# A recurrent mixer in chunks: matmuls of two row halves in turns, triangular inversions on GpSimd, a state held per head, and a convolution norm over four tiles

## The chip, the cores and the metric

The kernel runs on one core of one Trainium2 chip. The metric is the device time of one execution in microseconds (us). TensorE (PE in the profile), VectorE (DVE), ScalarE (ACT), GpSimd (POOL) and SyncE (SP, which here only starts DMAs) each work through a queue of their own, strictly in the order in which the program's scheduler has laid it out.

## The reference, cut to what matters

The kernel computes three blocks one after the other on a sequence of 1024 tokens with 1024 channels. The change touches the second block, and there two parts that both feed its output projection.

```python
# recurrent mixer: 8 heads of 64 channels, the state S of a head is 64 x 64
S = S * decay_t + v_t k_t' + (S a_t) b_t'          # one step per token
y_t = S r_t
# convolution part: 512 channels, after a causal convolution of 31 taps
mu  = mean(h, channels); var = mean((h - mu) ** 2, channels)
out = silu((h - mu) * rsqrt(var + 1e-5) * g + b)
```

The kernel replaces the steps over tokens by 8 chunks of 128 tokens, each of two blocks of 64. Within a block the term with `a_t` and `b_t` becomes the inverse of a unit triangular matrix.

## The kernel before, in words

`Block2.rwkv` (what the chunks run in) works in steps `i` from -3 to 8. A step weaves up to five generators, each for another chunk: `rwkv_chain(i)`, `rwkv_out(i-1)`, `rwkv_pre(i+1)`, `rwkv_solve(i+2)`, `rwkv_prep(i+3)`. In step -3 `conv_ln`, the norm of the convolution part, is woven in as well. The weaving only proposes an order: the scheduler of the tile framework fixes the order in each queue.

- `rwkv_prep` loads a chunk's r, k and v from DRAM (L1330), computes decays and scaled operands on ScalarE, GpSimd and VectorE (L1340 to L1388), and multiplies keys and queries of each head pair (L1403; the two heads of a pair lie on rows 0 to 63 and 64 to 127). VectorE masks the product into `gs` (L1405).
- `rwkv_solve` inverts 64 triangular matrices of 16 x 16 per chunk. Eight DMAs bring them from `gs` to DRAM (L1416), one brings them back with a matrix per partition (L1418), GpSimd copies them (L1423) and sets the diagonal (L1424), and 14 rounds follow, each a product (L1428) and a sum (L1430) on VectorE on [64, (15-t) x t] elements: 28 operations on 1120 elements per partition in all, each waiting for the one before. The inverse and its transpose (a copy, L1433) go back to DRAM (L1435, two DMAs) and by 16 DMAs into `tp` (L1439).
- `rwkv_pre` transposes (L1457), turns the 16 x 16 inverses into 64 x 64 ones (L1465, L1473) and applies them (L1480, L1488, L1493).
- `rwkv_chain` carries the state from block to block. The state `Tc` has a head pair in 128 rows by 64 columns. Before the output matmul (L1520) it is written twice scaled: by two operations of VectorE into a block-diagonal tile `Sbd` (L1516), and by one of GpSimd into `Sc` (L1518), which the next state is added to (L1534). L1522 adds the result to `X`, L1528 and L1539 are the matmuls of the state and the output, L1541 the output's copy.
- `rwkv_out` normalizes the output (L1553 to L1564; L1564 is on GpSimd), transposes it (L1568), adds the bonus term (L1572, GpSimd), gates it (L1576, L1577) and stores it.
- `conv_ln` works tile by tile on 128 tokens, 8 times: four transposes into a PSUM bank (L1212), statistics (L1215, L1217), an inverse square root by three Newton steps on a [128, 1] operand (L159 to L168), scaling from PSUM (L1221), transposes back (L1227), gain, SiLU (L1229 to L1234) and a store (L1235).

PSUM has 8 banks: one for `mm`, one for fillers (L172, a bfloat16 matmul that nothing reads), two for `s`, three for `t` (all of `pre` and `conv_ln`), one for `o` (the output of `chain`).

Of the kernel before, what the change touches and what calls it, by code (L numbers as in the profile page):

```python
# [8 lines left out]
F32 = mybir.dt.float32  # L9
# [3 lines left out]
AF = mybir.ActivationFunctionType  # L13
# [4 lines left out]
S = 1024  # L18
# [1112 lines left out]
RW = dict(chain=(9, "010000"), out=(4, "0000"), pre=(15, "100111011010001"), solve=(10, ""), prep=(7, "00010000001"), ln=16, weave=1)  # L1131


class Block2:
# [70 lines left out]
    def conv_ln(self, tmp):  # L1205
        c, nc = self.c, self.c.nc
        g, b = c.vecs["conv_ln_g"], c.vecs["conv_ln_b"]
        for t in range(8):
            ts = slice(t * 128, t * 128 + 128)
            q = c.psum("t")  # L1210
            for i in range(4):
                nc.tensor.transpose(q[:, 128 * i:128 * i + 128], self.cv[:, i, ts], c.ident)  # L1212
            yield
            st = c.sm([128, 6], pool=tmp)
            nc.vector.bn_stats(st, q)  # L1215
            mv = c.sm([128, 2], pool=tmp)
            nc.vector.bn_aggr(mv, st)  # L1217
            rs = c.sm([128, 1], tag="cl", pool=tmp)
# [1075 lines left out]
```

## Time and profile before

| | us |
|---|---|
| median of 3 runs | 3958.29 (3955.69 to 3967.6) |
| the profiled execution's own time | 3958.3 |
| its span, first to last instruction | 3956.6 |
| TensorE busy | 3795.8 (96%) |
| VectorE busy | 2112.9 (53%) |
| ScalarE busy | 1231.0 (31%) |
| GpSimd busy | 540.1 (14%) |
| mean granted TensorE clock | 0.970 of full speed |

A time in the profile counts from the first instruction. The stage of the change runs from about 1112 us (the projections' last matmul) to 1490 us (the first of a long row of matmuls of the output projection). The page's shares are means over the whole kernel, most of which is dense matmuls. The stage has to be read by itself: the busy time of each engine in it, what it idles for, and the order of each queue.

### The profile page before, as it was taken

Reading aid. Unit: us, or ns where it says so; the run is one execution under the profiler, and the core shown is the slowest. Engines: PE = TensorE matmul, PEld = TensorE weight load, DVE = VectorE, ACT = ScalarE, POOL = GpSimd, SP = SyncE. Lnnn points to the kernel's source line nnn. Section 1 sums busy time; section 2 is a strip of 40 time slices with the busy share of each in tenths; the row PEclk is TensorE's granted clock in tenths of the full one; section 3 lists DMA queues with packets and bytes.
Section 4 is the critical chain, followed back from the end, with each engine's and each line's share of the span. In section 5 each row is a group of like instructions: output and inputs, shape, how many; then the busy total and the mean of one; then the engine's idle time right before and its main releaser. Section 6 shows DMA issues by size and latency. Waiting matters only on the chain.

```text
span 3956.6 us, 52689 instructions
## 1 busy us (share of the span) xinstructions
PE 3795.8 (96%) x20288; PEld 3149.7 (80%) x20288; DVE 2112.9 (53%) x4845; ACT 1231.0 (31%) x2521; POOL 540.1 (14%) x825
## 2 busy tenths in 40 slices
PE   7999999799988989999999999999999999999998
PEld 6788888687867777888888888878788888888887
DVE  5356568678977865544444554444433443433155
ACT  4444435542233334222212242333322111121232
POOL 1011124300033411000000011111101211210000
PEclk9999998899978999999999999999999999999999
DMA  5321342431211133111111132111133222211143
GB/s 148 122 65 51 82 138 65 150 114 57 91 55 38 40 104 120 48 54 43 54 43 54 54 121 60 41 58 54 54 107 96 62 64 58 78 49 43 59 150 127
DMA packets 318636, 303.75 MB, mean 77 GB/s; under 512 B 50670, under 2 KB 260402, under 8 KB 318386
## 3 DMA queue, kind: packets, MB, share of 16 engines
q1 hardware_dynamic: 318386, 300.39, 24.5%
q8 instruction: 160, 2.62, 0.3%
q14 instruction: 90, 0.74, 0.1%
HBM read 234.27 MB, written 61.34 MB: 75 GB/s over the span
## 4 chain that ended last, share of the span: by engine, by line
PE 87%; DVE 6%; DMA 3%; ACT 1%; issue 1%; SPq 1%; POOL 1%; DVEq 0%; ACTq 0%; POOLq 0%
PE mm L251 71%; PE s L1809 2%; DMA wraw<-in_w_in_dram 1%; PE s L532 1%; PE t L568 1%; PE o L1831 1%; PE s L1990 1%; PE o L1883 1%; DVE ws L738 1%; PE t L213 1%; PE o L578 1%; PE o L579 1%; SPq L1439 1%; PE s L1403 0%; PE s L531 0%
## 5 line engine op out<-in xcount | busy, mean ns | idle before, releaser
L251 PE MATMUL mm<-ahi,whi 128*128 128x512 f32 x2464 | 967.2, 394 | 0.0
L251 PE MATMUL mm<-alo,whi 128*128 128x512 f32 x2464 | 965.5, 392 | 1.3 <-DVE alo L218 1.3
L251 PE MATMUL mm<-ahi,wlo 128*128 128x512 f32 x2464 | 964.3, 392 | 1.9 <-DVE wlo L184 1.9
L184 DVE TENSOR_TENSOR wlo<-wraw,whi 128x1024 fp32r<-128x1024 f32 (+2 forms) x300 | 358.2, 1231 | 361.1 <-PE mm L251 337.6
L251 PEld LDWEIGHTS mm<-ahi,wlo 128*128 128x128 f32 x2464 | 464.7, 189 | 98.4 <-DVE wlo L184 2.6
L251 PEld LDWEIGHTS mm<-ahi,whi 128*128 128x128 f32 x2464 | 465.8, 189 | 96.3 <-issue 0.4
L251 PEld LDWEIGHTS mm<-alo,whi 128*128 128x128 f32 x2464 | 465.1, 189 | 96.7 <-DVE alo L218 2.2
L183 ACT ACTIVATE whi<-wraw 128x1024 fp32r<-128x1024 f32 (+2 forms) x300 | 302.9, 1055 | 760.2 <-DMA wraw<-in_w_ff_dram 315.1
L251 PE MATMUL mm<-whi,ahi 128*128 128x512 f32 (+2 forms) x1088 | 400.2, 371 | 21.1 <-ACT whi L183 8.2
L251 PE MATMUL mm<-whi,alo 128*128 128x512 f32 (+2 forms) x1088 | 399.0, 368 | 1.6 <-DVE alo L218 1.6
L251 PE MATMUL mm<-wlo,ahi 128*128 128x512 f32 (+2 forms) x1088 | 400.4, 368 | 0.1
L251 PEld LDWEIGHTS mm<-whi,ahi 128*128 128x128 f32 x1088 | 206.6, 190 | 57.1 <-ACT whi L183 8.7
L1683 DVE TENSOR_TENSOR xm<-xm,mm 128x512 f32<-128x512 f32 x256 | 173.6, 684 | 119.8 <-PE mm L251 119.5
L251 PEld LDWEIGHTS mm<-wlo,ahi 128*128 128x128 f32 x1088 | 206.5, 190 | 35.2 <-issue 3.8
L251 PEld LDWEIGHTS mm<-whi,alo 128*128 128x128 f32 x1088 | 206.0, 189 | 35.2 <-issue 2.5
L251 PE MATMUL mm<-whi,ah 128*128 128x512 f32 x512 | 202.3, 395 | 0.0
L251 PE MATMUL mm<-wlo,ah 128*128 128x512 f32 x512 | 202.1, 395 | 0.0
L251 PE MATMUL mm<-whi,al 128*128 128x512 f32 x512 | 202.1, 395 | 0.0
L1170 DVE SCALAR_TENSOR_TENSOR cva<-cvh,vecs,cva 128x1022 f32<-128x1022 f32 (+29 forms) x120 | 145.4, 1262 | 0.2
L1665 DVE TENSOR_TENSOR fr<-fr 128x512 f32<-128x512 f32 x64 | 44.4, 694 | 154.0 <-ACT fr L1664 154.0
L207 POOL TENSOR_SCALAR x<-x,rT 128x1024 f32<-128x1024 f32 x16 | 20.9, 1307 | 752.3 <-PE mm L251 676.8
L1815 POOL TENSOR_SCALAR mS<-mS,s 128x256 f32<-128x256 f32 x128 | 60.8, 478 | 405.2 <-DVE s L1814 337.8
(576 smaller groups left out, 5761.2 us busy)
## 6 DMA issues: line engine op xcount, KB each, us to landing
wraw<-in_w_in_dram SPq DMA_DIRECT2D x41, 1024.0 KB
wraw<-in_w_ff_dram SPq DMA_DIRECT2D x32, 1024.0 KB
wraw<-in_w_in_dram SPq DMA_DIRECT2D x59, 512.0 KB
wraw<-in_w_out_dram SPq DMA_DIRECT2D x24, 1024.0 KB
gv<-go SPq DMA_DIRECT2D x32, 256.0 KB
vl<-gv SPq DMA_DIRECT2D x16, 512.0 KB
wraw<-in_w_proj_a_dram SPq DMA_DIRECT2D x8, 1024.0 KB
wraw<-in_w_proj_b_dram SPq DMA_DIRECT2D x8, 1024.0 KB
```

Source lines behind the costliest of these rows:

```text
L183: nc.scalar.activation(hi, src, AF.Copy)
L184: nc.vector.tensor_tensor(lo, src, hi.bitcast(F32), op=OP.subtract)
L213: nc.tensor.transpose(q[:, 128 * j:128 * j + 128], xn[:, (k + j) * 128:(k + j + 1) * 128], self.ident)
L251: nc.tensor.matmul(out, lhs[a][:, kl, ls], rhs[b][:, kr, rs], start=first and n == 0, stop=last and n == tot - 1)
L532: nc.tensor.matmul(q[:, :b - a], self.Q[0:64, h, qs], kl, start=False, stop=True)
L568: nc.tensor.transpose(t[:w, (2 * j + s) * 128:(2 * j + s + 1) * 128], Ps[s][:, k:k + w], c.ident)
L578: nc.tensor.matmul(o[:, :256], v[:w, 0:128], ph[:w, sl], start=first, stop=last, skip_group_check=True)
L1170: nc.vector.scalar_tensor_tensor(a[:, 30 - j:], h[:, 0:994 + j], wj, a[:, 30 - j:], op0=OP.mult, op1=OP.add)
L1665: nc.vector.tensor_tensor(r, r, r, op=OP.mult)
L1683: nc.vector.tensor_tensor(xm[t][:, ns], xm[t][:, ns], q, op=OP.add)
L1809: nc.tensor.matmul(q[:, :256], qk[:, a, qcol], qk[:, b, kcol], start=n == 0, stop=n == 2)
L1815: nc.gpsimd.tensor_scalar(S_, S_, r, 1.0, op0=OP.mult, op1=OP.mult)
```

## The change

Five edits, all in `Block2`:

1. Matmuls of two row halves are issued in turns, each half into a PSUM bank of its own (L1336, L1403, L1465, L1480, L1488 and L1493; L1344, L1411, L1474, L1491, L1500 and L1507 in the changed kernel).
2. The 28 operations of the inversion and the transposing copy go from VectorE to GpSimd (L1428, L1430, L1433; now L1437, L1439, L1442).
3. The block-diagonal `Sbd` goes. `Sc` is computed by VectorE and used as it is: four matmuls over 128 rows become eight over 64, with one bank for each of the two heads of a pair. The sum with `X` and the copy of the output are split in two as well.
4. `conv_ln` works on four tiles at a time: ScalarE copies the transposed tile to SBUF, the inverse square root is taken once for four tiles on a [128, 4] operand, and the scaling reads SBUF. In the weaving it has 24 places in step -3 in place of 16.
5. Banks: `t` has two in place of three, `o` two in place of one.

```diff
@@ conv_ln
-        for t in range(8):
...
-            c.rsqrt(rs, mv[:, 1:2], 1.0, 1e-5, "cl", tmp)
-            x = tmp.tile([128, 512], F32, tag="O", name=c.nm("lnx"), bufs=2)
-            nc.vector.tensor_scalar(x, q, mv[:, 0:1], rs, op0=OP.subtract, op1=OP.mult)
+        for t0 in (0, 4):
+            xs = []
+            mv = c.sm([128, 4, 2], tag="cmv", bufs=2, pool=tmp)
+            for k in range(4):
...
+                nc.scalar.activation(x, q, AF.Copy)
+                st = c.sm([128, 6], pool=tmp)
+                nc.vector.bn_stats(st, q)
+                nc.vector.bn_aggr(mv[:, k], st)
...
+            nc.vector.tensor_copy(vr, mv[:, :, 1])
+            c.rsqrt(rs, vr, 1.0, 1e-5, "cl", tmp)
+            for k, x in enumerate(xs):
...
+                nc.vector.tensor_scalar(x, x, mv[:, k, 0:1], rs[:, k:k + 1], op0=OP.subtract, op1=OP.mult)
@@ rwkv_prep
-            for s in range(2):
-                rs = slice(64 * s, 64 * s + 64)
-                q = c.psum("s")
-                for pr in range(4):
+            qq = [c.psum("s") for _ in half]
+            for pr in range(4):
+                for q, rs in zip(qq, half):
                     nc.tensor.matmul(q[:, 128 * pr:128 * pr + 128], kb[rs, pr, 2 * b:2 * b + 2], va[rs, pr, 1 + 4 * b:3 + 4 * b],
                                      start=True, stop=True)
+            for s, q in enumerate(qq):
                 TT(gs[:, b, s:8:2], r4(q), m, op=OP.mult)
@@ rwkv_solve
-            nc.vector.tensor_tensor(x, mv[:, t + 1:16, t:t + 1].to_broadcast(sh), tv[:, t:t + 1, 0:t].to_broadcast(sh),
+            nc.gpsimd.tensor_tensor(x, mv[:, t + 1:16, t:t + 1].to_broadcast(sh), tv[:, t:t + 1, 0:t].to_broadcast(sh),
                                     op=OP.mult)
-            nc.vector.tensor_tensor(tv[:, t + 1:16, 0:t], tv[:, t + 1:16, 0:t], x, op=OP.add)
+            nc.gpsimd.tensor_tensor(tv[:, t + 1:16, 0:t], tv[:, t + 1:16, 0:t], x, op=OP.add)
...
-        nc.vector.tensor_copy(lTT.rearrange("p (j t) -> p j t", t=16), tj)
+        nc.gpsimd.tensor_copy(lTT.rearrange("p (j t) -> p j t", t=16), tj)
@@ rwkv_pre
-        for b in range(2):
-            ca = slice(64 * b, 64 * b + 64)
-            q = c.psum("t")
-            for h in range(8):
-                nc.tensor.matmul(q[Bh(b), H(h)], gs[Bh(b), b, h, ca], T16[Bh(b), h], start=True, stop=True)
+        qq = [c.psum("t") for _ in range(2)]
+        for h in range(8):
+            for b, q in enumerate(qq):
+                nc.tensor.matmul(q[Bh(b), H(h)], gs[Bh(b), b, h, 64 * b:64 * b + 64], T16[Bh(b), h], start=True, stop=True)
+        for b, q in enumerate(qq):
             TT(ET[Bh(b), :, Bh(b)], h8(q[Bh(b)]), self.mLow[Bh(b)].unsqueeze(1).to_broadcast([64, 8, 64]), op=OP.mult)
@@ rwkv_chain
-                S = self.Sbd[b]
                 f = self.ff[j][:, :, b:b + 1]
-                for s in range(2):
-                    TT(S[H(s), :, H(s)], self.Tc[H(s)], f[H(s)].to_broadcast([64, 4, 64]), op=OP.mult)
                 Sc = tmp.tile([128, 4, 64], F32, tag="Sc", name=c.nm("Sc"), bufs=2)
-                nc.gpsimd.tensor_tensor(Sc, self.Tc, f.to_broadcast([128, 4, 64]), op=OP.mult)
-                for pr in range(4):
-                    nc.tensor.matmul(o[:, 128 * pr:128 * pr + 128], va[:, pr, 2 + 2 * b:4 + 2 * b], S[:, pr], start=pr == 0,
-                                     stop=False, skip_group_check=True)
-                TT(VU[b][Bh(b)], o[Bh(b)], X[Bh(b)], op=OP.add)
+                TT(Sc, self.Tc, f.to_broadcast([128, 4, 64]), op=OP.mult)
+                for pr in range(4):
+                    for s in range(2):
+                        nc.tensor.matmul(o[s][:, 64 * pr:64 * pr + 64], va[H(s), pr, 2 + 2 * b:4 + 2 * b], Sc[H(s), pr],
+                                         start=pr == 0, stop=False, skip_group_check=True)
+                for s in range(2):
+                    TT(hs(VU[b][Bh(b)], s), r4(o[s][Bh(b)]), hs(X[Bh(b)], s), op=OP.add)
@@ second_block
-        c.set_banks(mm=[0], f=[1], s=[2, 3], t=[4, 5, 6], o=[7])
+        c.set_banks(mm=[0], f=[1], s=[2, 3], t=[4, 5], o=[6, 7])
```

How the queues change is shown at three places. The first is GpSimd in a middle step, around the copy that begins an inversion. Before, only the copy (L1423) and the diagonal (L1424) of an inversion stood between operations of `prep`, `chain` and `out`:

```order
L1377 TENSOR_TENSOR ws_10869<-rk_12664,rk_12665 128x512
L1385 TENSOR_TENSOR ws_10873<-ws_10873,ws_10871 128x512
L1423 COPY ws_10872<-ws_10870 64x256
L1424 MEMSET ws_10872 64x16
L1345 TENSOR_SCALAR ws_10871<-rk_13112,vecs_625 128x128 x4
L1518 TENSOR_TENSOR Sc_13104<-Tc_12856,ff_11925 128x256
L1572 TENSOR_TENSOR y_12690<-y_12690,tp_11283 128x512
L1340 TENSOR_SCALAR ws_10871<-ws_10871 128x512
L1423 COPY ws_10872<-ws_10870 64x256
L1564 TENSOR_TENSOR O_12653<-O_12653,s_2559_13245 128x512
L1424 MEMSET ws_10872 64x16
```

Now the product and the sum of the 14 rounds stand there, with `out`'s normalization (L1582) among them:

```order
L1354 TENSOR_SCALAR ws_10871<-rk_13081,vecs_625 128x128
L1439 TENSOR_TENSOR ws_10872<-ws_10872,ws_10874 64x14
L1354 TENSOR_SCALAR ws_10871<-rk_13081,vecs_625 128x128 x3
L1437 TENSOR_TENSOR ws_10874<-ws_10870,ws_10872 64x26
L1439 TENSOR_TENSOR ws_10872<-ws_10872,ws_10874 64x13x2
L1437 TENSOR_TENSOR ws_10874<-ws_10870,ws_10872 64x36
L1439 TENSOR_TENSOR ws_10872<-ws_10872,ws_10874 64x12x3
L1437 TENSOR_TENSOR ws_10874<-ws_10870,ws_10872 64x44
L1439 TENSOR_TENSOR ws_10872<-ws_10872,ws_10874 64x11x4
L1437 TENSOR_TENSOR ws_10874<-ws_10870,ws_10872 64x50
L1582 TENSOR_TENSOR O_12151<-O_12151,s_2471_12758 128x512
L1439 TENSOR_TENSOR ws_10872<-ws_10872,ws_10874 64x10x5
```

Sixteen more operations of the same inversion and the bonus term of `out` (L1590) follow before the transposing copy, and only then `prep` of the next chunk.

The second place is SyncE's queue in a middle step (`tp` are the inverses, `gs` the products, `ws` the matrices by partition, `rk` the loads of a later chunk). Before:

```order
L1435 DMA lane<-ws_10872 64x256
L1435 DMA lane<-kb_10868 64x256
L1439 DMA tp_11283<-lane 16x8x16 x16
L1578 DMA catT<-y_13137 128x4x128
L1416 DMA lane<-gs_10867 16x8x16 x8
L1418 DMA ws_10870<-lane 64x256
```

Now, in the step of chunk 4:

```order
L1444 DMA lane<-ws_10872 64x256
L1444 DMA lane<-kb_10868 64x256
L1448 DMA tp_11221<-lane 16x8x16 x16
L1596 DMA catT<-y_12197 128x4x128
L1425 DMA lane<-gs_10866 16x8x16 x4
L1336 DMA rk_13080<-p2T 128x4x128
L1336 DMA rk_13081<-p2T 128x4x128
L1427 DMA ws_10870<-lane 64x256
```

The load that starts an inversion (L1427) stands behind the write-back and the 16 loads of the inversion before it. Of chunks 3 to 7, two had that load ahead of those 16 loads before (chunks 5 and 7, L1418 ahead of L1439); now all five have it behind. For chunk 2 it is ahead now and was behind before.

The third place is TensorE, where `prep` and `pre` of two chunks meet. Before, with the four groups of L1403 of a chunk (one bank `s` each):

```order
L1403 MATMUL s_12610<-va_10864,kb_10868 128x128 x4
L1576 MATMUL mm_12575<-lora,wup 128x128 x4
L1473 MATMUL t_12503<-Pc_12458,ws_10872 64x64 x16
L172 LDWEIGHTS reset
L172 MATMUL f_12522<-reset 128x384
L1403 MATMUL s_12616<-va_10864,kb_10868 128x128 x4
L1403 MATMUL s_12622<-va_10864,kb_10868 128x128 x4
L1488 MATMUL t_12529<-Pc_12520,ws_10870 64x64 x8
L1493 MATMUL t_12544<-X_2420_12299,Pc_12520 64x64 x8
L1488 MATMUL t_12582<-Pc_12520,ws_10870 64x64 x8
L1403 MATMUL s_12628<-va_10864,kb_10868 128x128 x4
```

Now, with the two groups of L1474 (banks `t`) and the first matmuls of L1411:

```order
L1474 MATMUL t_12707<-tp_11221,gs_10867 64x64 x8
L1536 MATMUL o_12775<-Sc_12776,va_10865 128x64 x4
L1411 MATMUL s_13022<-va_10864,kb_10868 128x128
L1474 MATMUL t_12708<-tp_11221,gs_10867 64x64 x8
L172 LDWEIGHTS reset
L172 MATMUL f_12726<-reset 128x384
L1545 MATMUL mm_12811<-ws_10870,ws_10874 64x64
L1556 MATMUL o_12774<-ws_10870,gs_10867 64x64 x4
L1411 MATMUL s_13023<-va_10864,kb_10868 128x128
L1545 MATMUL mm_12811<-ws_10870,ws_10874 64x64 x7
```

The product of keys and queries (L1411) alternates between its two banks at 77 of 127 neighbouring places, the low-rank product of `prep` (L1344) at 26 of 63. The two groups of L1474 still stand one behind the other, eight and eight, as L1465 did, and so do those of L1491 and L1507 in every chunk. L1500 alternates at 120 of 127 places.

## Rows read from the trace of the kernel before

**Rows 1.** The page: the span of the profiled execution.

```profile
span 3956.6 us, 52689 instructions
```

**Rows 2.** Busy time by stretch: us, then each engine, PEclk, DMA share, GB/s.

```profile
1110.00:1240.00 130.00, 100.58 (x658) 80.82 (x656) 91.27 (x242) 48.61 (x118) 55.91 (x74) 0.65 0.19 48
1240.00:1400.00 160.00, 149.21 (x1973) 126.26 (x1972) 136.88 (x328) 61.99 (x139) 62.63 (x83) 0.97 0.20 45
```

**Rows 3.** Chain of waits at the end of the stage: start us, us, what.

```profile
1490.83 9.37 PE mm L251 x28
```

**Rows 4.** SyncE's queue in order of time, whole stage: start us, us, what.

```profile
1178.98 0.49 SPq L1435 DMA_DIRECT2D lane<-ws  x1
...
1212.65 0.45 SPq L1435 DMA_DIRECT2D lane<-ws  x1
...
1241.09 0.45 SPq L1435 DMA_DIRECT2D lane<-ws  x1
...
1353.38 0.45 SPq L1435 DMA_DIRECT2D lane<-ws  x1
...
1356.31 8.11 SPq L1439 DMA_DIRECT2D tp<-lane  x16
...
1364.99 3.79 SPq L1416 DMA_DIRECT2D lane<-gs  x8
1369.93 0.47 SPq L1418 DMA_DIRECT2D ws<-lane  x1
...
1395.52 1.75 SPq L1416 DMA_DIRECT2D lane<-gs  x4
...
1434.93 0.45 SPq L1435 DMA_DIRECT2D lane<-ws  x1
```

**Rows 5.** Costly lines of VectorE, 1110 to 1490: busy us, mean ns | idle us.

```profile
L1430 DVE TENSOR_TENSOR ws<-ws,ws 64x14 f32<-64x14 f32 (+6 forms) x112 | 30.4, 271 | 2.5
L1428 DVE TENSOR_TENSOR ws<-ws,ws 64x14 f32<-64x14 f32 (+6 forms) x112 | 27.4, 245 | 13.0 <-POOL ws L1423 10.8
...
L1516 DVE TENSOR_TENSOR Sbd<-Tc,ff 64x256 f32<-64x256 f32 x30 | 16.5, 551 | 0.4
...
L164 DVE SCALAR_TENSOR_TENSOR cl<-cl,cl 128x1 f32<-128x1 f32 x24 | 10.4, 432 | 0.1
```

**Rows 6.** GpSimd in order of time, 1340 to 1410: start us, us, what.

```profile
1343.35 0.63 POOL L1518 TENSOR_TENSOR Sc<-Tc,ff 128x256 f32<-128x256 f32 x1 [1.37 <-DVE Tc L1534]
...
1359.42 1.40 POOL L1345 TENSOR_SCALAR ws<-rk,vecs 128x128 f32<-128x128 f32 x4
...
1372.39 0.60 POOL L1423 COPY ws<-ws 64x256 f32<-64x256 f32 x1 [1.61 <-DMA ws<-lane]
1373.17 1.04 POOL L1564 TENSOR_TENSOR O<-O,s 128x512 f32<-128x512 f32 x1 [0.18 <-DVE s L168]
...
1375.75 0.12 POOL L1424 MEMSET ws<- 64x16 f32 x1
1375.90 1.04 POOL L1361 TENSOR_TENSOR ws<-ws,s 128x512 f32<-128x512 f32 x1
...
1388.19 1.26 POOL L1572 TENSOR_TENSOR y<-y,tp 128x512 f32<-128x512 f32 x1 [0.78 <-ACT y L1570]
```

**Rows 7.** VectorE in order of time, one operation of an inversion.

```profile
1375.93 1.05 DVE L1430 TENSOR_TENSOR ws<-ws,ws 64x14 f32<-64x14 f32 x1
```

**Rows 8.** The copy ahead of the inversions (L1423): ns min/median/max, first and last start us.

```profile
L1423 POOL COPY ws<-ws x8: 597/608/1214, 1153.1 to 1406.7; 64x256 f32<-64x256 f32 x8
```

**Rows 9.** TensorE in order of time, 1354 to 1361.

```profile
1354.81 1.14 PE L1480 MATMUL t<-ws,gs 64*64 64x64 f32 x16
...
1356.74 1.15 PE L1473 MATMUL t<-Pc,ws 128*64 128x64 f32 x32
...
1359.05 1.71 PE L1403 MATMUL s<-va,kb 64*128 64x128 f32 x16
```

**Rows 10.** Waits of TensorE, 1110 to 1490: us in total, times, longest us.

```profile
PE mm L1568 <- POOL O L1564: 6.7, 1, 6.7
```

More of the change, by code (lines that the diff above doesn't have):

```diff
@@ L1130 @@
 FN = 384
-RW = dict(chain=(9, "010000"), out=(4, "0000"), pre=(15, "100111011010001"), solve=(10, ""), prep=(7, "00010000001"), ln=16, weave=1)
+RW = dict(chain=(9, "010000"), out=(4, "0000"), pre=(15, "100111011010001"), solve=(10, ""), prep=(7, "00010000001"), ln=24, weave=1)
 class Block2:
@@ L1331, in rwkv_prep @@
         sg, a, cs, kk, e, ei, ea, t1, t2, t3 = self.wk[:10]
-        for x, rows, b in ((sg, slice(0, 64), "w0"), (a, slice(64, 128), "a0")):
-            q = c.psum("s")
-            for pr in range(4):
-                ps = slice(128 * pr, 128 * pr + 128)
+        half = [slice(0, 64), slice(64, 128)]
+        qq = [c.psum("s") for _ in half]
+        for pr in range(4):
+            ps = slice(128 * pr, 128 * pr + 128)
+            for q, rows in zip(qq, half):
                 nc.tensor.matmul(q[:, ps], self.wup[rows, 0, ps], self.lwa[rows, js], start=True, stop=True)
+        for x, q, b in ((sg, qq[0], "w0"), (a, qq[1], "a0")):
             for pr in range(4):
@@ L1476, in rwkv_pre @@
             yield
[L1477 to L1478 removed]
+            if i == 0:
+                qq = [c.psum("t") for _ in range(2)]
                 for h in range(8):
[L1480 to L1482 removed]
+                    for b, q in enumerate(qq):
+                        nc.tensor.matmul(q[Bh(b), H(h)], gs[Kh(b), b, h, Kh(b)], VU[b][Kh(b), H(h)], start=True, stop=True)
+                for b, q in enumerate(qq):
+                    nc.scalar.activation(x1[Bh(b)], q[Bh(b)], AF.Copy)
+                    yield
         X = self.X[j] = tmp.tile([128, 512], F32, tag="X", name=c.nm("X"), bufs=2)
[L1484 to L1487 removed]
+        qq = [c.psum("t") for _ in range(2)]
+        for h in range(8):
+            pr, s = h // 2, h % 2
+            for b, q in enumerate(qq):
                 nc.tensor.matmul(q[H(s), H(pr)], VU[b][Bh(b), H(h)], cur[Bh(b), H(h)], start=True, stop=True)
+        for b, q in enumerate(qq):
             nc.scalar.activation(va[:, :, 3 + b], q[:, 0:256].rearrange("p (r t) -> p r t", r=4), AF.Copy)
             yield
[L1491 to L1492 removed]
+        qq = [c.psum("t") for _ in range(2)]
+        for h in range(8):
+            for b, q in enumerate(qq):
                 nc.tensor.matmul(q[Bh(b), H(h)], cur[Bh(b), H(h)], x1[Bh(b), H(h)], start=True, stop=True)
+        for b, q in enumerate(qq):
             nc.scalar.activation((X if j or b else VU[b])[Bh(b)], q[Bh(b)], AF.Copy)
@@ L1538, in rwkv_chain @@
             for h in range(8):
-                nc.tensor.matmul(o[Kh(b), H(h)], gs[:, b, h, cr], VU[b][:, H(h)], start=first and h == 0, stop=h == 7,
-                                 skip_group_check=True)
-            nc.scalar.activation(O[Kh(b)], o[Kh(b)], AF.Copy)
+                pr, s = h // 2, h % 2
+                nc.tensor.matmul(o[s][Kh(b), 64 * pr:64 * pr + 64], gs[:, b, h, cr], VU[b][:, H(h)], start=first and pr == 0,
+                                 stop=pr == 3, skip_group_check=True)
+            for s in range(2):
+                nc.scalar.activation(hs(O[Kh(b)], s), r4(o[s][Kh(b)]), AF.Copy)
             yield
```

77 lines of the change are left out of this document (32 added, 45 removed).

## The prediction

> **What bounds the kernel now.** I read the page first: the span is 3956.6 us [rows 1], and 3958.3 us is the same execution's own time, equal to the median of the three runs (3958.29), so every sum below is made against it. Its shares say nothing of this change, since dense matmuls fill most of the span. So the table of busy times by stretch comes next [rows 2]. From 1240 to 1400 us VectorE is busy 136.88 of 160 us and TensorE 149.21 (its ends are modelled, so it is less full than that), GpSimd only 62.63. In the 130 us ahead of it the granted clock is 0.65: TensorE is at 1.2 GHz for much of the time, while it waits for VectorE and GpSimd; later it is 0.97, nearly always 2.4 GHz. The stage ends where the long row of dense matmuls begins, at 1490.83 [rows 3].
>
> Third I read SyncE's queue, since a chunk's inversion goes out and in through it, and take the start of the write-back (L1435) as the clock of the stage [rows 4]. Call it T. It starts at 1179.0 for chunk 0, 1212.7, 1241.1 and so on, and 1434.9 for chunk 7: 36.6 us per chunk. From T(7) to the end of the stage are 55.9 us.
>
> **The change, part by part.**
>
> *Inversions leave VectorE.* Their 224 operations take 30.4 + 27.4 us there [rows 5], 7.2 us of each chunk. In the middle VectorE is busy 136.88 / 160 x 36.6 = 31 us per chunk, so this is a real relief.
>
> *Inversions on GpSimd.* No row shows a small tensor-tensor operation there, so I bound it. Below: a fill of 16 elements takes 0.12 us. Above: 256 elements in a copy take 0.60. An operation with two inputs takes 1.04 on 512 [rows 6]. The line through 0.60 and 1.04 has 1.72 ns per element and 0.16 us fixed. 28 operations with 1120 elements: 28 x 0.16 + 1120 x 0.00172 = 6.4 us, and 28 gaps of 0.05 (0.03 stands between the fill and what follows) make 7.8. I take that line because it passes between the bounds and fits both kinds. The bounds are 3.4 and 16.8 us. Copy and fill ahead: 0.72. The queue puts other work among the 28: four scalings for the next chunk (1.40), out's normalization (1.04) and bonus sum (1.26), 3.7 in all.
>
> *The shared port.* GpSimd's operation at 1375.90 to 1376.94 [rows 6] and a 14-element sum of VectorE from 1375.93, which took 1.05 us [rows 7], ended together: the small one waited for the big one. So 28 small reads of SBUF beside VectorE's sums of two SBUF operands will meet. I estimate 2.0 us per inversion, a 0.7 us operation met one time in ten. The Trainium skill, page "SBUF — State Buffer", section "Who interferes with whom", says that a VectorE instruction with two SBUF inputs and a GpSimd instruction that reads SBUF exclude each other fully; the trace agrees with the 1.05 us above.
>
> The Trainium skill, "GPSIMD Engine Reference", section 3.1, speaks against this part: elementwise work with two inputs is about twice as slow on GpSimd. By that rule one operation costs twice VectorE's 0.245 to 0.271 us, an inversion 14.4 us in place of 9.8, and the time would be 7 x 4.6 = 32 us above my sum, 3950; no run here shows it.
>
> *The new loop.* The queue order sets what is late next. The load that starts chunk j+1's inversion stands behind chunk j's write-back and its 16 loads. From rows [rows 4, 6]: T to the first of the 16, 1356.31 - 1353.38 = 2.93; the 16, 8.11; to the next issue 0.57; four DMAs of `gs` 1.75; two loads of a later chunk, 2 x 0.45 like their neighbours; from the end of the `gs` DMAs (1368.78) to the load at 1369.93, 1.15; to GpSimd's copy at 1372.39, 2.46. Together 17.9. Then GpSimd: 0.72 + 7.8 + 3.7 + 2.0 = 14.2. The loop is **32.1 us per chunk**, for the five from T(2) to T(7). prep's own operations on GpSimd fit into the 17.9: it is busy 62.63 / 160 x 36.6 = 14.3 per chunk, less 4.3 for two state scalings (0.63), out's two and the copy, so 10.0.
>
> *The start.* T(0): the copy ran at 1153.1 [rows 8], behind the norm's work in GpSimd's queue, and it still does. Then came 26 us to T(0); now there are 0.7 + 7.8 + 2.0 and 10.0 of the next prep, 20.5 us, with two tiles of the norm and waits on top. I leave T(0) at 1179, within 10 us either way. T(1) = T(0) + 33.7 as before. Chunk 2's load no longer waits for the 16, and its inversion follows at once: 10.0 + 0.7 + 7.8 + 2.0 + 0.6 = 21.1, so T(2) = 1233.8. T(7) = 1233.8 + 5 x 32.1 = 1394.3, **40.6 us** ahead of 1434.9.
>
> *The norm over four tiles.* It removes three quarters of the Newton steps; the 24 of L164 alone took 10.4 us [rows 5] for single elements. All lie in the first 70 us, where T(0) hangs on GpSimd's queue: I count nothing. If that cover is gone, T(0) comes up to 10 us earlier; the two `t` banks can take as much back.
>
> *State per head.* VectorE loses two operations of 0.55 per block [rows 5] and gains one, and a split sum; ScalarE gains a copy. About 1 us per chunk, hidden by the loop; without that cover it is 8 us in all.
>
> *Row halves.* In the trace L1473 alternates column halves: 32 instructions in 1.15 us, where L1480, with its half fixed for eight matmuls, takes 1.14 for 16; L1403 takes 1.71 for 16 [rows 9]. Turns halve the time. But the order gives L1474, L1491 and L1507 no turns, L1411 77 of 127, L1344 26 of 63. At 0.107 us each L1403's 256 instructions are 27 us and L1336's 128 are 14: 27 x 0.61 / 2 + 14 x 0.41 / 2 = 11 us of TensorE in the whole stage instead of the 48 that full turns would give (with 9 each for L1465, L1480 and L1493). By the same rows the matmuls of one chunk need 27 us at full clock (116 instructions of 128 columns at 0.107, 128 of 64 at 0.071, 160 in turns at 0.036), fillers apart. That was under the loop before and stays under 32.1, so I count nothing; up to 11 us if TensorE sets the pace.
>
> *The tail* after T(7) keeps its 55.9. **Sum: 3958.3 - 40.6 = 3918 us.** The bounds of the small operation alone give 3880 (3.4 us in place of 7.8 and no meeting at the port, in the six inversions from T(1) to T(7)) and 3981 (16.8 in place of 7.8, in all seven).
>
> **The rivals.**
>
> *The loads cost less than I think* and the engines set the pace: VectorE needs 31 - 7.2 - 1 = 23 us, TensorE 26 and its fillers. Steps of 28 and a T(0) 10 us earlier put T(7) at 1223.8 + 140 = 1363.8, 71 us ahead: 3887. For it: SyncE idles much of the time. Against it: the queue order.
>
> *TensorE stalls.* Its transposes of the output wait for GpSimd (6.7 us once [rows 10]), and in two or three steps the normalization now stands a dozen places into an inversion. TensorE waits in order, its clock falls to 1.2 GHz as in the first stretch (0.65 [rows 2]), and pre, which follows the inversion, runs at half speed. Steps of 38, about the 38.8 that these five took before, with T(2) unchanged at 1241: T(7) = 1431, 3954: no change.
>
> *Slower: GpSimd becomes the bound through the port.* If half the 28 operations wait for a 0.7 us operation, the 2.0 becomes 9.8: loop 40, T(1) and T(2) 8 later each. T(7) = 1249.8 + 200 = 1450, 15 late, and VectorE's own sums wait as well, some 3 us: 3976. It decides from 40.6 / 7 = 5.8 us more per inversion, a mean of 0.56 us per operation, inside my bounds.
>
> *The turns don't happen* (the order says so for three of the six lines) takes TensorE's relief from the second case; it leaves the sum as it is.
>
> **How the numbers follow.** A measurement of this kernel tells 0.3% (12 us) from no change. The forecast, 3918, has 0.50; engine-bound, 3887, 0.22; the stall, 3954, 0.16; slower, 3976, 0.12. The first two are faster by more than 12 us: 0.72; same 0.16; slower 0.12. The range reaches from the lower bound of the small operation, which takes in the second case, past the third: 3880 to 3962. What lies above is the fourth.
>
> **What would show it.** Right: write-backs about 32 us apart from chunk 2 on, each copy 18 us behind the write-back before it; 28 operations of 0.2 to 0.35 us on GpSimd; VectorE's busy time in the middle down by a quarter; T(7) near 1394. L1411 faster, L1474 not. Wrong: small operations at 0.5 us or more; GpSimd waiting for ScalarE or VectorE inside an inversion; a clock clearly below 0.97 after chunk 1; copies that start as soon as GpSimd is free, which would mean that the loads don't set the pace.

## The result, and the profile after

The changed kernel takes 0.9941 of the time before (95% interval 0.9924 to 0.9957), 23 us less of 3959; its executions lie between 3927.8 and 3944.62 us; one in a slow state, 7285.15 us, is left out. The profiled one took 3944.62 us, its span against [rows 1]:

```profile
span 3942.9 us, 52905 instructions
```

So the profile has 13.7 us of the 23 to show. The stage itself shortened by more. Three windows of busy time (us, PE, PEld, DVE, ACT, POOL, then PEclk, DMA share, GB/s): the dense matmuls ahead of the stage, with the same code in both kernels, and the stage from its first matmul of prep to the end, first before,

```profile
779.00:1110.00 331.00, 325.98 (x1450) 268.93 (x1451) 275.53 (x457) 93.77 (x169) 16.94 (x18) 0.99 0.28 93
1117.00:1491.00 374.00, 317.42 (x3433) 264.44 (x3433) 278.42 (x704) 140.59 (x310) 132.89 (x172) 0.83 0.23 58
```

then after, with the two stretches of [rows 2] between them:

```profile
779.00:1110.00 331.00, 321.27 (x1416) 264.73 (x1417) 271.00 (x453) 94.92 (x169) 16.13 (x17) 0.97 0.29 96
1110.00:1240.00 130.00, 107.31 (x899) 88.06 (x899) 79.02 (x146) 57.47 (x135) 84.19 (x157) 0.74 0.23 59
1240.00:1400.00 160.00, 154.32 (x1951) 128.27 (x1948) 105.66 (x211) 61.16 (x146) 99.80 (x222) 0.90 0.22 50
1125.00:1481.00 356.00, 315.94 (x3550) 260.61 (x3549) 214.58 (x432) 146.11 (x334) 193.48 (x389) 0.83 0.24 61
```

By 1110 the profiled execution of the changed kernel is 34 dense matmuls (7.6 us, at 325.98 / 1450 each) behind, before any changed line has run. The stage takes 356 us in place of 374. VectorE lost 64 us, GpSimd gained 61. TensorE has hardly fewer busy microseconds (315.94 against 317.42) though the halves now take turns, and in the middle its clock is lower than before (0.90 against 0.97). So nearly all of the 18 us is idle time of TensorE, 57 us before and 40 after.

The clock of the stage that the prediction used, the write-back of each chunk, in SyncE's queue (start us, us, what), chunks 2 to 7, with the next inversion's load where the loop is read:

```profile
1242.75 0.45 SPq L1444 DMA_DIRECT2D lane<-ws  x1
...
1273.19 0.45 SPq L1444 DMA_DIRECT2D lane<-ws  x1
...
1288.72 0.47 SPq L1427 DMA_DIRECT2D ws<-lane  x1
...
1307.88 1.35 SPq L1444 DMA_DIRECT2D lane<-ws  x1
...
1338.10 0.45 SPq L1444 DMA_DIRECT2D lane<-ws  x1
...
1372.16 0.45 SPq L1444 DMA_DIRECT2D lane<-ws  x1
...
1400.89 0.45 SPq L1444 DMA_DIRECT2D lane<-ws  x1
```

From T(2) to T(7) are 158.1 us, 31.6 per chunk (28.7 to 34.7 in the single steps). GpSimd in order of time, a copy that waits for its load and the last inversion from end to end:

```profile
1291.28 0.60 POOL L1432 COPY ws<-ws 64x256 f32<-64x256 f32 x1 [3.41 <-DMA ws<-lane]
...
1391.50 0.21 POOL L1437 TENSOR_TENSOR ws<-ws,ws 64x14 f32<-64x14 f32 x1
...
1396.22 0.28 POOL L1437 TENSOR_TENSOR ws<-ws,ws 64x56 f32<-64x56 f32 x1
1396.58 0.30 POOL L1439 TENSOR_TENSOR ws<-ws,ws 64x56 f32<-64x56 f32 x1
...
1400.65 0.22 POOL L1439 TENSOR_TENSOR ws<-ws,ws 64x14 f32<-64x14 f32 x1
```

What follows T(7) is where the forecast parts from the trace. TensorE in order of time: the first matmuls of chunk 7 that need its inversion (L1474) run only at 1425.29, and until then TensorE works through chunk 6, chain and dense matmuls, with one gap of 0.49 us. Behind these rows stands the end of the stage, in the chain of waits (start us, us, what).

```profile
1417.22 1.14 PE L1507 MATMUL t<-X,Pc 64*64 64x64 f32 x16 [0.49 <-ACT va L1502]
...
1425.29 1.14 PE L1474 MATMUL t<-tp,gs 64*64 64x64 f32 x16
```

```profile
1480.81 19.32 PE mm L251 x78
```

In the kernel before 55.9 us lay between T(7) and 1490.83 [rows 3, 4]; here it is 1480.81 - 1400.89 = 79.9. TensorE's busy time in these two stretches, before and after (columns of the windows above), shows that the 24 us more are work and not waits: it is idle for 11.7 us in either.

```profile
1434.00:1491.00 57.00, 45.35 (x527) 38.45 (x526) 27.44 (x69) 20.86 (x38) 10.05 (x9) 0.90 0.30 89
1400.00:1481.00 81.00, 69.32 (x779) 56.75 (x776) 35.80 (x84) 29.49 (x55) 9.50 (x11) 0.86 0.27 89
```

The lines of TensorE that the change touches (busy us, mean ns | idle us before), after:

```profile
L1411 PE MATMUL s<-va,kb 64*128 64x128 f32 x256 | 30.9, 344 | 8.8 <-DVE cl L166 6.0 <-DVE cl L1226 2.8
L1536 PE MATMUL o<-Sc,va 64*128 64x64 f32 x240 | 25.9, 292 | 0.2 <-DVE Sc L1533 0.2
L1556 PE MATMUL o<-ws,gs 128*64 128x64 f32 x256 | 25.9, 255 | 0.0
L1474 PE MATMUL t<-tp,gs 64*64 64x64 f32 x256 | 20.7, 247 | 0.0
L1491 PE MATMUL t<-ws,gs 64*64 64x64 f32 x256 | 20.3, 233 | 0.0
L1545 PE MATMUL mm<-ws,ws 128*64 128x64 f32 x240 | 18.0, 261 | 4.1 <-DVE ws L1539 4.1
L1507 PE MATMUL t<-X,Pc 64*64 64x64 f32 x256 | 17.9, 221 | 1.8 <-ACT va L1502 1.8
L1344 PE MATMUL s<-lora,wup 64*128 64x128 f32 x128 | 14.4, 317 | 0.1
L1500 PE MATMUL t<-Pc,ws 64*64 64x64 f32 x256 | 5.6, 224 | 0.5 <-DVE Pc L1485 0.5
```

and those of them in the kernel before that had most to change (the others there: L1465 22.5, L1480 20.3, L1493 17.8, L1488 10.9, L1528 11.9 us):

```profile
L1403 PE MATMUL s<-va,kb 64*128 64x128 f32 x256 | 38.2, 333 | 2.6 <-DVE gs L1405 1.1 <-DVE cl L168 0.9 <-DVE kb L1388 0.6
L1336 PE MATMUL s<-lora,wup 64*128 64x128 f32 x128 | 23.4, 332 | 0.0
L1539 PE MATMUL o<-ws,gs 128*64 128x64 f32 x256 | 20.9, 236 | 0.0
L1520 PE MATMUL o<-Sbd,va 128*128 128x128 f32 x120 | 19.5, 309 | 0.0
```

The six lines of the halves fell from 133.1 to 109.8 us. The three of the chain (L1520, L1528, L1539; now L1536, L1545, L1556) rose from 52.3 to 69.8. So the chain took back 17.5 of the 23.3 us. Only 6.4 of the 17.5 lie in the line whose matmuls doubled (L1520, now L1536); the other two lines have as many matmuls as before.

### The profile page after: what moved, and what is told of

Same layout as the page of the kernel before. It is cut to its first block, busy times and chain, and to the rows that moved or that the text cites. A ratio compares the mean times of both kernels' runs of the same rounds, so it can differ in the third digit from the quotient of the medians.

```text
span 3942.9 us, 52905 instructions
## 1 busy us (share of the span) xinstructions
PE 3804.1 (96%) x20408; PEld 3155.7 (80%) x20408; DVE 2049.9 (52%) x4573; ACT 1237.7 (31%) x2545; POOL 602.4 (15%) x1041
## 4 chain that ended last, share of the span: by engine, by line
PE 89%; DVE 5%; DMA 3%; ACT 1%; issue 1%; POOL 1%; SPq 0%; DVEq 0%; ACTq 0%; POOLq 0%
PE mm L251 72%; PE s L1827 2%; DMA wraw<-in_w_in_dram 1%; PE s L532 1%; PE t L568 1%; PE s L2008 1%; PE o L1849 1%; PE o L1901 1%; DVE ws L738 1%; PE t L213 1%; PE t L1483 1%; PE o L578 1%; PE o L579 1%; PE s L531 0%; PE t L1474 0%
```

## The experiments

The four parts of the change were first tried one at a time in the kernel before (the banks go with the state per head). Then the state per head and the inversions were each taken out of the changed kernel, and its fillers and the order of its turns were varied; the norm and the halves were not taken out of it. Two theories stand against each other in what was expected. T: TensorE sets the step of the changed kernel. I: the loop of write-back, loads and inversion still does. In the table us is (ratio - 1) x 3960. The stage's length and TensorE's busy time are those of each profile's window, as above; idle is the rest of the window; "at 1.2 GHz" is 2 x (1 - PEclk) x length, good to 4 us. The last column is the mean step of the write-backs from T(2) to T(7). A ratio is to executions of the kernel before taken beside that kernel. The changed kernel was not run again beside its variants, so a difference between two rows compares two ratios.

| kernel | ratio to before (95%) | us | stage | TensorE busy | idle | PEclk | at 1.2 GHz | step |
|---|---|---|---|---|---|---|---|---|
| before | 1 | 0 | 374 | 317 | 57 | 0.83 | 127 | 38.8 |
| changed | 0.9941 (0.9924 to 0.9957) | -23 | 356 | 316 | 40 | 0.83 | 121 | 31.6 |
| b_inv: before + inversions | 0.9949 (0.9933 to 0.9966) | -20 | 364 | 322 | 42 | 0.81 | 138 | 35.0 |
| b_norm: before + norm | 0.9975 (0.9961 to 0.9989) | -10 | 367 | 311 | 56 | 0.84 | 117 | 31.7 |
| b_state: before + state per head | 1.0094 (1.0075 to 1.0113) | +37 | 407 | 354 | 53 | 0.78 | 179 | 39.6 |
| b_rows: before + halves in turns | 0.9925 (0.9907 to 0.9942) | -30 | 345 | 289 | 56 | 0.88 | 83 | 32.4 |
| b_t2: before, two t banks | 1.0000 (0.9989 to 1.0012) | 0 | 373 | 313 | 60 | 0.84 | 119 | 33.3 |
| b_rowsnorm: before + halves + norm | 0.9970 (0.9958 to 0.9982) | -12 | 363 | 305 | 58 | 0.83 | 123 | 32.3 |
| a_nostate: changed, old chain | 0.9900 (0.9883 to 0.9918) | -40 | 338 | 289 | 49 | 0.87 | 88 | 33.4 |
| a_invdve: changed, inversions on VectorE | 1.0031 (1.0019 to 1.0043) | +12 | 386 | 341 | 45 | 0.80 | 154 | 36.8 |
| a_turns: changed, turns held in order | 1.0011 (0.9999 to 1.0023) | +4 | 386 | 293 | 93 | 0.81 | 147 | 35.1 |
| a_nofill: changed, no fillers | 1.0057 (1.0042 to 1.0073) | +23 | 401 | 322 | 79 | 0.75 | 200 | 38.5 |
| s_fill: b_state, more fillers | 1.0071 (1.0059 to 1.0083) | +28 | 409 | 358 | 51 | 0.81 | 155 | 38.9 |
| ns_fill: a_nostate, more fillers | 0.9992 (0.9983 to 1.0001) | -3 | 375 | 328 | 47 | 0.83 | 128 | 38.0 |

**The inversions alone (b_inv).** The operations of L1428, L1430 and L1433 of the kernel before:

```
-            nc.vector.tensor_tensor(x, ...)
-            nc.vector.tensor_tensor(tv[:, t + 1:16, 0:t], ...)
-        nc.vector.tensor_copy(lTT..., tj)
+            nc.gpsimd.tensor_tensor(x, ...)
+            nc.gpsimd.tensor_tensor(tv[:, t + 1:16, 0:t], ...)
+        nc.gpsimd.tensor_copy(lTT..., tj)
```

> The kernel before with nothing changed but the inversions, which run on GpSimd. Theory T (in the changed kernel TensorE's own work sets the step of about 33 us, and the inversions only release it up to there): the loop of the write-backs falls from 36.6 to about 32 us, but TensorE, which here has the halves in blocks, needs 33 us or more a step, so the time falls by 5 to 15 us. Theory I (the loop of the inversions still sets the pace in the changed kernel, and the other parts add nothing): the whole gain of the change, 23 us, is here.

Measured: 20 us less (13 to 27), near the 23 of the whole change, as theory I has it; but what the other parts gave (next runs) is far from nothing, so this run alone decides neither. TensorE's idle time in the stage fell from 57 to 42 us. The step of the write-backs fell to 35.0 us only, not to the 32 that was expected, T(2) and T(7) being

```profile
1246.94 0.45 SPq L1435 DMA_DIRECT2D lane<-ws  x1
...
1421.99 0.45 SPq L1435 DMA_DIRECT2D lane<-ws  x1
```

**The norm alone (b_norm).** `conv_ln` and the weaving number as in the change:

```
-        for t in range(8):
+        for t0 in (0, 4):
+            for k in range(4):
...
+            c.rsqrt(rs, vr, 1.0, 1e-5, "cl", tmp)
...
- ln=16
+ ln=24
```

> The kernel before with nothing changed but the convolution's norm over four tiles (and its 24 turns). The prediction counts it as nothing: within 6 us of the kernel before, with the first write-back within 10 us of 1179. Rival: its Newton steps were on VectorE's path at the start, and the time falls by 10 us.

Measured: 10 us less, the rival's figure. The term was not nothing. That the Newton steps were on the path is not shown by it: T(0) comes at 1171.32, within the 10 us that the prediction allowed, and TensorE's idle time in the stage is what it was (57 and 56 us); its busy time is 6 us less.

**The state per head alone (b_state).** `rwkv_chain` and the banks as in the change:

```
-                    nc.tensor.matmul(o[:, 128 * pr:128 * pr + 128], va[:, pr, ...], S[:, pr], ...)
+                    for s in range(2):
+                        nc.tensor.matmul(o[s][:, 64 * pr:64 * pr + 64], va[H(s), pr, ...], Sc[H(s), pr], ...)
...
-        c.set_banks(mm=[0], f=[1], s=[2, 3], t=[4, 5, 6], o=[7])
+        c.set_banks(mm=[0], f=[1], s=[2, 3], t=[4, 5], o=[6, 7])
```

> The kernel before with nothing changed but the state per head (two o banks, two t banks). The prediction counts it as nothing: within 6 us. Rivals: VectorE's 1 us per chunk is on the path and the time falls by 8 us; or the third t bank was needed, and pre, which takes its PSUM there, makes it slower by 5 to 15 us.

Measured: 37 us more, outside every expectation; the profiled execution, 3989.16 us, is the shortest of its six, so its profile shows less than that. Its busy time by stretch:

```profile
1220.00:1240.00 20.00, 20.00 (x269) 16.71 (x268) 17.47 (x55) 10.06 (x25) 8.56 (x17) 1.00 0.26 58
1240.00:1260.00 20.00, 20.00 (x151) 17.16 (x151) 18.34 (x50) 3.76 (x7) 4.37 (x7) 0.52 0.19 47
1260.00:1280.00 20.00, 20.00 (x177) 16.75 (x177) 6.71 (x12) 5.19 (x16) 5.75 (x9) 0.50 0.14 17
1280.00:1300.00 20.00, 20.00 (x113) 14.96 (x114) 13.58 (x42) 4.53 (x9) 4.36 (x5) 0.50 0.08 20
1300.00:1320.00 20.00, 20.00 (x230) 16.61 (x231) 8.95 (x16) 3.94 (x9) 2.70 (x5) 0.78 0.09 18
```

For these 100 us TensorE is busy all the time, and for 68 of them (2 x (1 - PEclk) x 20 in each window) the granted clock is 1.2 GHz. At full clock the same work takes a little over half as long by the price below, so this one stretch costs up to 34 us. The list of waits names none for TensorE from 1220 to 1310: nothing kept it from working. Its last idle time before the fall lies between 1200 and 1220, where it is busy for 17.77 of 20 us. Its order of time shows what it ran as the clock fell (start us, us, what), and the price of L1462's 16 matmuls there, 1.80 and 1.97 us, where the changed kernel's same line at full clock (L1474, above) takes 1.14:

```profile
1237.37 1.10 PE L1518 MATMUL o<-Sc,va 64*128 64x64 f32 x8
...
1240.43 1.80 PE L1462 MATMUL t<-tp,gs 64*64 64x64 f32 x16
...
1297.25 1.97 PE L1462 MATMUL t<-tp,gs 64*64 64x64 f32 x16
```

**The halves in turns alone (b_rows).** The loops of `rwkv_prep` and `rwkv_pre` as in the change, one of six:

```
-        for b in range(2):
-            q = c.psum("t")
-            for h in range(8):
-                nc.tensor.matmul(q[Bh(b), H(h)], gs[Bh(b), b, h, ca], T16[Bh(b), h], ...)
+        qq = [c.psum("t") for _ in range(2)]
+        for h in range(8):
+            for b, q in enumerate(qq):
+                nc.tensor.matmul(q[Bh(b), H(h)], gs[Bh(b), b, h, 64 * b:64 * b + 64], T16[Bh(b), h], ...)
```

> The kernel before with nothing changed but the loops over row halves written in turns. Theory T: in the kernel before the loop of the inversions, 36.6 us, stands above TensorE's work, so less TensorE work gives nothing, within 6 us. Rival: TensorE is on the path already, and its 11 us less are 11 us of time.

Measured: 30 us less, more than the whole change. TensorE is busy 28 us less, and 44 us fewer of the stage run at 1.2 GHz; its idle time is what it was. The six lines of the halves have 26 of the 28: they take 107.2 us in place of 133.1. So TensorE was on the path of the kernel before, against theory T's reading of it and against the prediction. The step of the write-backs fell too, from 38.8 to 32.4 us, with the inversions still on VectorE:

```profile
1239.56 0.45 SPq L1438 DMA_DIRECT2D lane<-ws  x1
...
1401.63 0.45 SPq L1438 DMA_DIRECT2D lane<-ws  x1
```

**Two t banks (b_t2).**

```
-        c.set_banks(mm=[0], f=[1], s=[2, 3], t=[4, 5, 6], o=[7])
+        c.set_banks(mm=[0], f=[1], s=[2, 3], t=[4, 5], o=[7])
```

> The kernel before with nothing changed but the banks of PSUM: two t banks in place of three. Two readings of the 37 us by which the state per head alone made the kernel slower. Banks: its third t bank was what pre needed, so this kernel loses 20 to 37 us as well, and the granted clock is at 1.2 GHz for some 180 us of the stage in place of 133. Chain: the new chain itself (sixteen half-row matmuls in place of eight whole ones, VectorE's scaling in the chain) costs it, and this kernel is within 8 us of the kernel before.

Measured: no difference. The third t bank is not what the state per head costs, which leaves the new chain; its two o banks by themselves were not tried. The run shows one thing more. T(7) comes 24.9 us earlier than in the kernel before, at

```profile
1410.01 0.45 SPq L1435 DMA_DIRECT2D lane<-ws  x1
```

and the stage still ends at 1492 in place of 1491. An earlier last inversion is not by itself time.

**The changed kernel without the state per head (a_nostate).** The edit of b_state taken back:

```
-        c.set_banks(mm=[0], f=[1], s=[2, 3], t=[4, 5], o=[6, 7])
+        c.set_banks(mm=[0], f=[1], s=[2, 3], t=[4, 5, 6], o=[7])
...
+        self.Sbd = cut(S0, 2)
...
-                        nc.tensor.matmul(o[s][:, 64 * pr:64 * pr + 64], va[H(s), pr, ...], Sc[H(s), pr], ...)
+                    nc.tensor.matmul(o[:, 128 * pr:128 * pr + 128], va[:, pr, ...], S[:, pr], ...)
```

> The changed kernel with the chain, the block-diagonal state and the banks of the kernel before: inversions on GpSimd, halves in turns and the norm over four tiles remain. If the parts add up (0.9949 x 0.9975 x 0.9925 = 0.985 of the time before): 59 us below the kernel before, about 36 below the changed kernel. If inversions and turns relieve the same path (each step needs both shorter): no better than the turns alone with the norm, 30 to 40 us below the kernel before. By the clock: the time at 1.2 GHz within the stage falls from 126 us in the changed kernel to 90 or less.

Measured: 40 us less than before and 16 less than the changed kernel (7 to 26, both intervals taken together). It has the shortest time of all, 10 us (0 to 20) below the halves alone. The state per head costs 16 us in this company and 37 alone, so the parts do not add. TensorE's busy time fell from 316 to 289 us and the time at 1.2 GHz from 121 to 88 us, the latter as expected.

**Turns held in order (a_turns).** For each of the six loops:

```
+    def turn(self, first, ins):
+        if not first:
+            self.tc.keep_in_program_order(ins)
...
-                nc.tensor.matmul(q[Bh(b), H(h)], cur[Bh(b), H(h)], x1[Bh(b), H(h)], start=True, stop=True)
+                c.turn(h == 0 and b == 0, nc.tensor.matmul(q[Bh(b), H(h)], cur[Bh(b), H(h)], x1[Bh(b), H(h)], start=True, stop=True))
```

> The changed kernel with every matmul of the six loops over halves, but the first of each loop, held in program order on TensorE, so that the turns that the program writes are there. Theory T (TensorE's work sets the step of 33 us): L1474, L1491 and L1507 take 1.1 us per 16 at full clock in place of 0.6, L1411 and L1344 about half, some 3 us of the step: 15 to 30 us below the changed kernel. Theory I (the loop of write-back, loads and inversion, 31.6 us, is close behind): 8 us at most. If the order held costs TensorE waits that the free order avoided: no gain, and waits on VectorE and ScalarE of over 10 us appear on TensorE.

Measured: 28 us above the changed kernel, the third case, though no single wait reaches the 10 us that it names. (The expectation has two figures the wrong way round: 0.6 us per 16 was to take the place of 1.1.) The turns are there, and they do save TensorE work (lines of TensorE, columns as above):

```profile
L1512 PE MATMUL t<-X,Pc 64*64 64x64 f32 x256 | 15.4, 269 | 4.4 <-ACT va L1507 4.4
L1496 PE MATMUL t<-ws,gs 64*64 64x64 f32 x256 | 13.2, 243 | 1.7 <-DVE Pc L1490 1.6
L1479 PE MATMUL t<-tp,gs 64*64 64x64 f32 x256 | 12.5, 245 | 0.0
```

20.7, 20.3 and 17.9 us have become 12.5, 13.2 and 15.4, and TensorE as a whole is busy 23 us less. Its idle time rose by 53, though. The longest waits (us in total, times, longest) are

```profile
PE t L1488 <- ACT X L1498: 9.7, 2, 9.4
PE s L1406 <- POOL ws L1390: 9.6, 2, 6.8
```

where the longest single one in the changed kernel is 6.0. That whatever stands behind a pinned matmul waits with it would explain this, but no run shows it apart from the rest; the time at 1.2 GHz rose as well, by 26 us.

**Without fillers (a_nofill).** The fillers' products are never used.

```
-RW = dict(chain=(9, "010000"), out=(4, "0000"), pre=(15, "100111011010001"), solve=(10, ""), prep=(7, "00010000001"), ...
+RW = dict(chain=(9, ""), out=(4, ""), pre=(15, ""), solve=(10, ""), prep=(7, ""), ...
```

> The changed kernel without the eleven filler matmuls per chunk (L172; their products are never used). Theory T: they are 3 to 5 us of TensorE in a step of 33, so the time falls by 20 to 30 us if the granted clock stays as it is. Rival: the fillers hold the clock up, the time at 1.2 GHz grows from 126 us of the stage to 160 or more, and the kernel is 10 to 20 us slower. Theory I: within 8 us.

Measured: 46 us above the changed kernel, the rival, and more than it said. The 88 fillers' 32.5 us of TensorE are gone and TensorE's busy time is still 6 us longer, since some 200 us of the stage run at 1.2 GHz. These are 79 more than in the changed kernel, which at half the clock are up to 40 us of busy time, so the clock can account for it:

```profile
1125.00:1526.00 401.00, 322.19 (x3457) 277.39 (x3453) 214.54 (x432) 146.96 (x333) 191.58 (x389) 0.75 0.21 54
```

**Inversions back on VectorE (a_invdve).** The edit of b_inv, the other way round, in the changed kernel:

```
-            nc.gpsimd.tensor_tensor(x, ...)
+            nc.vector.tensor_tensor(x, ...)
...
```

> The changed kernel with the inversions back on VectorE; the rest of the change remains. If the parts add up, as the inversions alone gave 0.9949: the time rises from 0.9941 to 0.999 of the kernel before, 20 us above the changed kernel. If halves in turns and inversions relieve the same path, and TensorE sets the step in the changed kernel: within 8 us of the changed kernel.

Measured: 36 us above the changed kernel (28 to 44). Without the move the other three parts together are 12 us slower than the kernel before, so the gain hangs on it. How it does is not what the prediction had: of the 30 us by which the stage is longer, 25 are busy time of TensorE and 5 are idle, so the run does not show TensorE waiting for the inversions. The time at 1.2 GHz is 33 us longer, which can make up to 17 of the 25.

**Halves and norm, nothing else (b_rowsnorm).** a_nostate with the same edit:

```
-            nc.gpsimd.tensor_tensor(x, ...)
+            nc.vector.tensor_tensor(x, ...)
...
```

> Halves in turns and the norm over four tiles alone: the inversions are on VectorE, the chain is that of the kernel before. If these two add up (0.9925 x 0.9975 = 0.990): as fast as with the inversions on GpSimd (a_nostate, 0.990), so that the inversions are worth nothing once the halves take turns. If the inversions are worth their 20 us there too: 0.995 of the kernel before, some 3943 us.

Measured: 0.9970, neither of the two. Against a_nostate the inversions are worth 28 us (19 to 36) here. And the norm, 10 us of gain in the kernel before, is 18 us of loss on top of the halves (10 to 26).

**More fillers (s_fill, ns_fill).** s_fill is b_state with more fillers in the chain, ns_fill is a_nostate with more in chain, prep and norm:

```
-chain=(9, "010000")
+chain=(9, "111111")
```

```
-chain=(9, "010000"), prep=(7, "00010000001")
+chain=(9, "010100"), prep=(7, "01010101001")
...
-                gens.append((self.conv_ln(tmp), RW["ln"]))
+                gens.append((self.filled(self.conv_ln(tmp), "1" * 24), RW["ln"]))
```

> The kernel with the state per head alone, with a filler matmul at each of the six steps of the chain in place of one. If the granted clock is what costs its 37 us (TensorE fully busy at 1.2 GHz from 1241 to 1309): the time at 1.2 GHz in the stage falls from 181 us to 140 or less, and the kernel is 15 us or more below 4002. If it is TensorE's longer work: five fillers a chunk, 0.3 us each, are 12 us more, 4014.

> The changed kernel without the state per head (a_nostate, 0.990 of the time before) and with more fillers: one at each of the norm's 24 steps, three more in prep and one more in the chain per chunk. Clock: the time at 1.2 GHz in the stage falls from 88 us to 65 or less and the kernel is 5 to 12 us below a_nostate. Work: the fillers are 24 x 0.4 + 8 x 4 x 0.3 = 19 us of TensorE, and the kernel is up to 19 us above a_nostate.

Measured: s_fill is 9 us below b_state (0 to 18), with 24 us less at 1.2 GHz and longer TensorE work, between its two cases; of the two profiled executions that of s_fill is the longer, by 5 us, so the profiles do not show the 9. ns_fill is 36 us above a_nostate, twice the 19 us that its fillers were to cost TensorE, and its time at 1.2 GHz grew by 40 us. A filler is held in order behind everything written before it, as the matmuls of a_turns are; that this is why more of them lowered the clock is not shown.

## Why the prediction was right, and where its working was not

The time, 0.9941 of before, lies 17 us above the 3918 forecast, inside the range and on the forecast side. Step by step:

**The new loop: right in its length, but not shown to set the time.** Forecast 32.1 us per chunk from T(2) to T(7), measured 31.6. Both halves are right: from T to the copy were to be 17.9 and are 16.5 to 18.1 (T(3) = 1273.19 to 1291.28 above is the longest), and three of the five copies wait for their load; from the copy to the next T were to be 14.2 and are 14.3 in the mean. T(7) was to come 40.6 us earlier; it comes 34.0 earlier in a profile that entered the stage 7.6 late. But the move alone does not give that step. Taken back it lengthens the step to 36.8 (a_invdve), yet alone it gives 35.0 (b_inv), and steps of 32.4 and 31.7 come without it (b_rows, b_norm), so the step answers to other work as well. And b_t2 has a T(7) 24.9 us earlier for no gain at all, so the sum's rule, that an earlier T(7) is as much less time, does not hold.

**The operations on GpSimd: right in sum, not in make-up.** 7.8 us and 2.0 for the port were forecast. The last inversion runs undisturbed, from 1391.50 to 1400.87, in 9.4 us: the gaps are 0.08 and not 0.05, and an operation takes 0.21 us at 14 elements and 0.28 to 0.30 at 56. All 224 took 67.1 us, 0.30 each, against 0.26 on VectorE [rows 5]: a ratio of 1.16. The Trainium skill, "GPSIMD Engine Reference", section 3.1, has such work about twice as slow on GpSimd; for operations this small the trace does not agree. The rival's 3950 lies as near to the measured time, some 3935, as 3918 does, so it is these durations that decide against it.

**The price of the move: near in number, not in mechanism.** 40.6 us were forecast. The move is worth 20 alone (b_inv), 28 beside halves and norm (a_nostate against b_rowsnorm), and 36 when it is taken back (a_invdve), and of the 30 us that the profiles show of these 36, 25 are busy time of TensorE and not the wait for inversions that the 40.6 stand for. That the forecast came near is in part luck.

**The tail keeps its 55.9: wrong.** It became 79.9, by 24 us of TensorE's work. This is the step that failed. Behind it is "that was under the loop before and stays under 32.1, so I count nothing": TensorE's 27 us per chunk left out the fillers (32.5 us over the stage, 4 per chunk) and every microsecond at 1.2 GHz (121 of the stage). TensorE's steps are 33 us (L1474 starts at 1193.6 for chunk 0 and at 1425.29 for chunk 7), so pre of chunk 7 follows chunk 6 on TensorE and not T(7), and of the 34 us that the inversions are early, 10 are left at the end.

**State per head, counted as nothing: wrong, and alone the largest miss.** The prediction weighed VectorE's two operations for one and a copy of ScalarE. It did not count TensorE. Alone the edit costs 37 us, in the change 16. The doubled matmuls by themselves need not cost that. At full clock the sixteen of a block take 1.11 us in one place, and eight of them 1.10 in another, against 1.05 for the old eight (first the kernel before, then twice the changed one):

```profile
1444.39 1.05 PE L1520 MATMUL o<-Sbd,va 128*128 128x128 f32 x8
```

```profile
1360.67 1.10 PE L1536 MATMUL o<-Sc,va 64*128 64x64 f32 x8
...
1460.71 1.11 PE L1536 MATMUL o<-Sc,va 64*128 64x64 f32 x16
```

That the first sixteen alternate between the halves and the eight do not is inferred from these prices. The larger part is the clock: the 52 us more at 1.2 GHz in b_state make up to 26 of its 36 us more of busy time.

**Row halves, counted as nothing: wrong.** The order did foretell which lines gain (L1403's 38.2 us became 30.9, L1336's 23.4 became 14.4; L1465's 22.5 is still 20.7). The "11 us of TensorE" are half of the 23.3 that the six lines lost; they leave out L1488, which alternates too and went from 10.9 to 5.6. That none of it would be seen was wrong: alone it is 30 us. In the changed kernel the chain's growth takes most of TensorE's relief back. These two misjudged terms offset each other, and that a sum that left both out came close is luck.

**The norm, counted as nothing: wrong by 10 us** in the kernel before, and of the other sign beside the halves.

**The rivals.** "Engine-bound" named the right engine (TensorE) with too short a step, 28 for 33. "TensorE stalls" had the falling clock, but put it down to waits, and b_state shows a fall with none. The port did not become the bound: 18 of the 224 operations took over 0.4 us. The prediction's own test "a clock clearly below 0.97 after chunk 1" came out against it: 0.90.

**What stays open.** Over the fourteen kernels the stage's length goes with the time at 1.2 GHz, about 0.6 us of stage for each (a line through the table's columns, which does not say which of the two is the cause); only in b_state's stretch and in a_nofill is it plain that the clock is the cause. What in the order of the matmuls makes the clock fall, and so why the norm helps in one kernel and hurts in another, no run here settles. Every edit also lets the scheduler lay the queues out anew, and no run keeps the order apart from the edit. Inversions and halves without the norm and the state per head were not tried, nor turns held in order without the state per head, nor another place for the fillers.

## What to carry to other kernels

Where a loop on one engine is to be shortened, work out the step of the next engine with everything in it, fillers and slow-clock time too, before its slack is counted on: here the loop came out to within 0.5 us, and more than half of its gain was gone between the last inversion and the end. An earlier last write-back is not time unless the engine behind it was waiting for it. Work out TensorE's side, in turns and out of turns and at either clock, for any edit that looks like a saving on VectorE. And test a bundle of edits with each one taken out: the shortest time here is that of the change without one of its four parts.

## What the runs showed of the hardware that was not expected

- TensorE's granted clock fell to 1.2 GHz while the engine was busy all the time and waited for nothing (b_state, from 1241, 20.00 of 20 us in each window), and it stayed there for 68 us. The Trainium skill, "TensorE: Matmul & The Clock Gate", Part 1, ties the lower clock to an engine that has been idle; in this stretch the trace shows no idle time, only short matmuls, many of them on 64 rows, and fillers. The profile models the ends of matmuls, so gaps shorter than one would not show.
- Taking 88 matmuls away from TensorE (a_nofill) lengthened its busy time in the stage, from 316 to 322 us, through the clock (200 us of the stage at 1.2 GHz in place of 121).
- Small operations with two inputs cost on GpSimd nearly what they cost on VectorE: 0.30 us against 0.26, a mean over sizes from 14 to 56 elements on 64 rows.
- The order of matmuls on half the rows sets their price: L1474's 256 took 20.7 us in blocks of one half, and 12.5 us (L1479) when held in turns, though more of that kernel's stage ran at 1.2 GHz (a_turns, 147 us against 121).
